# A two-layer decoder trunk in 32-bit split arithmetic: attention scores issued at another place, and the norm's row made by plain 32-bit matmuls

## The chip, the cores and the metric

The kernel runs on one NeuronCore of one Trainium2 chip. The metric is the device time of one launch in microseconds (us), as the median of several executions. All times below are in us unless they are marked ns. Engines go by the short names of the profile: PE is TensorE (matmuls), PEld its weight loads, DVE is VectorE, ACT is ScalarE, POOL is GpSimd, SP is SyncE, which issues the DMAs.

## The reference

One sequence of 256 tokens, width 2048, two layers, everything in float32:

```python
for i in range(2):
    a = rmsnorm(h, attn_norm[i])
    h = h + (sb_dilated_mixer if i == 0 else fox_mixer)(a, ...)      # 16 heads of 128
    h = h + conv_ffn(rmsnorm(h, ffn_norm[i]), ...)                   # 2048 -> 2*5632 -> 2048
    gate = sigmoid(rmsnorm(h, ple_norm[i]) @ w_ple_gate[i])
    h = h + gate * (p[i] @ w_ple[i])
return rmsnorm(h, final_norm)
```

Layer 0 has 8 stick-breaking heads (the weight of a key is a product of the "not taken" shares of the keys after it, computed with a suffix sum) and 8 dilated heads with rotary positions (softmax). Layer 1 has 16 forgetting heads (softmax with a bias from cumulated forget gates).

## The kernel before, in words

**The arithmetic.** A 32-bit weight is split in two float32r parts: ACT copies it rounded (L165), DVE subtracts that copy from the original (L166). Activations are kept in two such parts as well. A product of the two takes three float32r matmuls per 128 x 128 block (`PARTS`: high by high, high by low, low by high). Small matmuls of attention take their operands as plain float32 instead and are recorded twice in the trace for each matmul.

**The stream of weights.** All weights come through one list, cut into units of mostly 4 blocks of 128 rows by 256 columns. SP loads groups of units into the raw tile `wr` (3 buffers), ACT and DVE split a unit into `w` (4 buffers), PE uses it in 24 matmuls of 256 columns. `unit` keeps three split units ahead of PE.

**The order of the work.** `gemm_unit` and `gemm_v` call `tick()` after every unit. `defer(n, fn)` puts a small job into a list that `tick` runs n units later, so that attention stands between units of the large products. A scheduler then orders the instructions on each engine, on the whole as they were written.

**A head pair** (`head_pair`, 8 per layer) makes the queries (`psq`, 4 units, weights stationary, activations moving), the keys (`psk`, 4 units, likewise) and the values (`psv`, 4 units; `gemm_v` at L229 to L240, where the activations are stationary and the weights move). Its attention has three steps that PE takes part in: `first` makes the scores `scs` (stick-breaking: L428, L431 in `sb_first`; softmax: L472, L474, and in layer 1 also L470, in `sm_first`); `second`, 5 units later (stick-breaking, L450 to L455) or 4 units later (softmax, the transposes of L509), makes `sps`; `attend`, 2 units after that, makes `avp` (L518, L520). Between the three, DVE and ACT work on the scores: masks, exponentials, sums. In layer 1 each pair is followed by one short unit, `psp` (12 matmuls, weights stationary, `ple_up`). The first pair of layer 1 makes its values first, together with the forget gates (`gemm_vf`, L250).

In the kernel before, `first` is deferred by 2 units after the keys, or by 3 in layer 0 where rotary positions have to be applied (pairs 4 to 7). So the scores stand inside the four units of `psv`, at the half or after the third unit. In the first pair of layer 1, where no `psv` follows, they stand in the next `psq` instead.

**The norm.** `norm_sums` adds the squares over partitions by matmuls (`nps`, L291) and finds the factor per token, `rT`, by small DVE steps. `norm_rows` spreads it as a row over all partitions: the identity times `rT` (`nd`, L314) is multiplied by a matrix of ones into `rps`, and DVE copies the row to `rb` (L325). Before the change, six of the seven norms split `nd` in two float32r parts, `ndh` by ACT (L321) and `ndl` by DVE (L322), and add two float32r matmuls of 256 columns (L324). The last norm (`mixer is None`) takes two plain 32-bit matmuls of 128 columns each (L316).

Of the kernel before, what the change touches and what calls it, by code (L numbers as in the profile page):

```python
# [10 lines left out]
F32 = mybir.dt.float32  # L11
F32R = mybir.dt.float32r
# [5 lines left out]
P = 128  # L18
D = 2048
S = 256  # L20
# [36 lines left out]
def _cuts(n):  # L57
    return (4, 4, n // 2 - 4, n // 2 - 4) if n != 16 else (4, 4, 4, 4)
# [46 lines left out]
def trunk(ctx: ExitStack, tc: tile.TileContext, xT, pT, pos, gains, conv, bf, cst, wst, out):  # L105
    nc = tc.nc
# [19 lines left out]
    ones = ct[:, C_ONE:C_ONE + 128]  # L126

    def mm_tile(name):
        return psum.tile([P, 2, S], F32, name=name, tag="mm", bufs=4)

    def at_tile(name):
        return psum.tile([P, 2, 512], F32, name=name, tag="at", bufs=2)

    def t2_tile(name, shape=(P, 2, S), dt=F32):
        return work.tile(list(shape), dt, name=name, tag="t2", bufs=6)
# [46 lines left out]
    def defer(n, fn):  # L182
        later.append((at["tick"] + n, fn))
# [24 lines left out]
    def gemm(ps, act, kind, l, c0, cuts, k0=0, koff=0, part=None):  # L208
        n = len(cuts)
        for i, kc in enumerate(cuts):  # L210
            if part is None or i in part:
                gemm_unit(ps, act, kind, l, c0, k0, i == 0, i == n - 1, koff)
            k0 += kc
# [28 lines left out]
    def gemm_vf(ps, act, l):  # L242

        n = 256 + NH
        for k0, kc in VF_CUTS:
            _, w = unit("w_vf", l, k0, 2 * D)
            for t in range(2):
                for k in range(kc):
                    for i, (a, b) in enumerate(((0, 0), (0, 1), (1, 0))):
                        nc.tensor.matmul(ps[:, t, :n], lhsT=act[:, k0 + k, a, t * P:(t + 1) * P],  # L250
                                         rhs=w[:, k, b, :], start=k0 + k + i == 0,
                                         stop=k0 + k == KT - 1 and i == 2)
            tick()
# [55 lines left out]
    def norm_rows(mixer):  # L309

        dg = t2_tile("nd", (P, 2, P))
        ps = at_tile("rps")
        for t in range(2):
            nc.vector.tensor_scalar_mul(out=dg[:, t, :], in0=ident, scalar1=rT[:, t:t + 1])  # L314
            if mixer is None:
                nc.tensor.matmul(ps[:, 0, t * P:(t + 1) * P], lhsT=ones, rhs=dg[:, t, :],  # L316
                                 start=t == 0, stop=True, skip_group_check=True)
        if mixer is None:
            return ps[:, 0, :S]
        dh, dl = t2_tile("ndh", (P, 2, P), F32R), t2_tile("ndl", (P, 2, P), F32R)  # L320
        nc.scalar.copy(out=dh, in_=dg)  # L321
        nc.vector.tensor_sub(out=dl, in0=dg, in1=dh.bitcast(F32))  # L322
        for i, x in enumerate((dh, dl)):
            nc.tensor.matmul(ps[:, 0, :S], lhsT=trir[:, 0, :], rhs=x, start=i == 0, stop=i == 1)  # L324
        nc.vector.tensor_copy(out=rb, in_=ps[:, 0, :S])  # L325
        if mixer:
            nc.vector.tensor_scalar_mul(out=rq, in0=rb, scalar1=SCALE)
# [6 lines left out]
    def with_rows(fn):  # L334

        if at["rows"] > at["tick"]:
            later.append((at["rows"], fn))
        else:
            fn()
# [30 lines left out]
    trir = cpool.tile([P, 2, P], F32R, name="trir")  # L370
# [76 lines left out]
    def sb_second(z, e, eh, el):  # L447
        sp = at_tile("sps")
        for i, x in enumerate((eh, el)):
            nc.tensor.matmul(sp[:, 0, :], lhsT=trir[:, 1, :], rhs=x[:, 0:512],  # L450
                             start=i == 0, stop=False, skip_group_check=True)
            nc.tensor.matmul(sp[:, 1, 0:256], lhsT=trir[:, 1, :], rhs=x[:, 512:768],
                             start=i == 0, stop=i == 1, skip_group_check=True)
        for i, x in enumerate((eh, el)):
            nc.tensor.matmul(sp[:, 0, :].rearrange("p (j c) -> p j c", j=2)[:, :, 128:256],  # L455
                             lhsT=trir[:, 0, :], rhs=x[:, 512:768].rearrange("p (j c) -> p j c", j=2),
                             start=False, stop=i == 1, skip_group_check=True)
        nc.vector.tensor_sub(out=z, in0=z, in1=sp.rearrange("p a b -> p (a b)")[:, :768])
        nc.scalar.activation(out=e, in_=z, func=AF.Exp)
        return e  # L460
# [107 lines left out]
    def head_pair(l, hp, act, dst, st):  # L568
        q = work.tile([P, 2, S], F32, name="q", tag="qkv", bufs=2)
        k = work.tile([P, 2, S], F32, name="k", tag="qkv", bufs=2)  # L570
        v = work.tile([P, 2, S], F32, name="v", tag="v", bufs=1)
        full = _cuts(KT)
        if l % 2 == 1 and hp == 0:
            ps = at_tile("psv")
            gemm_vf(ps, act, l)
            for t in range(2):
                nc.scalar.activation(out=v[:, t, :], in_=ps[:, t, 0:S], func=AF.Copy,
                                     scale=rT[:, t:t + 1])
            st["fox"] = forget_gates(l, ps)
        ps = mm_tile("psq")  # L580
        gemm(ps, act, "w_in", l, hp * 256, full)
        with_rows(lambda ps=ps: nc.vector.tensor_mul(out=q, in0=ps, in1=rq2))
        ps = mm_tile("psk")
        gemm(ps, act, "w_in", l, D + hp * 256, full)
        nc.vector.tensor_mul(out=k, in0=ps, in1=rb2)

        def first():
            if l % 2 == 0 and hp < 4:
                a = sb_first(q, k)
                defer(5, lambda: second(lambda: sb_second(*a)))  # L590
            else:
                a = sm_first(q, k, st["fox"] + (2 * hp,) if l % 2 == 1 else None)
                defer(4, lambda: second(lambda: sm_second(*a)))

        def second(fn):
            w = fn()
            defer(2, lambda: attend(hp, w, v, dst))

        if l % 2 == 0 and hp >= 4:
            rope(q)  # L600
            rope(k)
        defer(2 + (l % 2 == 0 and hp >= 4), first)
        if l % 2 == 1 and hp == 0:
            return
        ps = mm_tile("psv")
        gemm_v(ps, act, l, 2 * D + hp * 256)
        for i in range(2):
            nc.scalar.activation(out=v[:, i, :], in_=ps[:, i, :], func=AF.Copy, scale=rT[:, i:i + 1])
# [29 lines left out]
    for l in range(DEPTH):  # L638
# [51 lines left out]
        for op in range(8):  # L690
            end = l + 1 == DEPTH and op == 7
            if end:
                ws = [unit("w_ple_gate", l, 4 * i, op * 256)[1] for i in range(4)]
                ps = [at_tile("pse")[:, j, :S] for j in range(2)]
            else:
                ps = mm_tile("psg")
# [15 lines left out]
            else:  # L712
                more = []
                for j in range(2):
                    for k in range(KT):
                        for n, (a, b) in enumerate(((0, 0), (0, 1), (1, 0))):
                            nc.tensor.matmul(ps[j],  # L717
                                             lhsT=ws[k // 4][:, k % 4, a, j * P:(j + 1) * P],
                                             rhs=X[:, k, b, :], start=k == 0 and n == 0,
                                             stop=k == KT - 1 and n == 2)  # L720
# [98 lines left out]
```

## Time and profile before

| | |
|---|---|
| median of 3 runs | 2430.46 (2429.55 to 2431.67) |
| the profiled execution's own time | 2430.3 |
| its span, first to last instruction | 2428.5 |
| PE busy | 2406.8 (99%), 20974 matmuls |
| DVE, ACT busy | 1595.8 (66%), 1228.6 (51%) |
| DMA | 458.06 MB, mean 189 GB/s |

The page's busy time of PE counts the modelled length of matmuls that overlap one another (276 ns each in the psu group), so it is not the rate at which they follow. The timeline merges the matmuls of one line into a row with the start of the first, the time to the end of the last, and their count; the difference between the starts of two rows that follow each other, divided by the count of the first, is the time that one matmul took of PE.

### The profile page before, as it was taken

The page shows a single profiled execution, that of the slowest core. Times are in us where ns is not written, and L with a number is a line of the kernel's source. Part 1 is how long each engine was busy: PE and PEld are TensorE (multiplying, and loading weights), DVE is VectorE, ACT ScalarE, POOL GpSimd, SP SyncE. Part 2 cuts the span into 40 slices and gives each one's busy share as a digit, 9 for nine tenths or more (in the row PEclk, how much of TensorE's full clock was granted, in tenths as well). Part 3 has the DMA queues.
Part 4 walks back from the last instruction along what each step waited for, and adds up shares of the span by engine and source line. Part 5 has one row for each costly group of instructions (what it writes and reads, how often), then busy time and mean ns, then how long its engine had stood idle before and what let it go on. Part 6 is the DMA issues. An engine that isn't in the chain of part 4 may idle for free.

```text
span 2428.5 us, 47969 instructions
## 1 busy us (share of the span) xinstructions
PE 2406.8 (99%) x20974; PEld 2400.7 (99%) x20974; DVE 1595.8 (66%) x2157; ACT 1228.6 (51%) x1549; POOL 2.5 (0%) x8
## 2 busy tenths in 40 slices
PE   8999999999999999999999999999999999999997
PEld 8999999999999999999999999999999999999997
DVE  7557666776567657767765555667665776667676
ACT  6554455554355445555554444555544554455553
POOL 0000000000000000000000000000000000000000
PEclk9999999999999999999999999999999999999998
DMA  7444445555555555555455445555555555555553
GB/s 269 174 174 174 170 178 191 192 195 198 197 191 191 187 200 196 197 185 204 176 184 181 170 170 167 199 191 198 193 191 192 193 198 191 201 191 187 193 196 120
DMA packets 66484, 458.06 MB, mean 189 GB/s; under 512 B 7409, under 2 KB 7425, under 8 KB 16609
## 3 DMA queue, kind: packets, MB, share of 16 engines
q1 hardware_dynamic: 66096, 454.53, 53.0%
q8 instruction: 164, 2.69, 0.4%
q0 software_dynamic: 176, 0.46, 0.1%
q14 instruction: 48, 0.39, 0.0%
HBM read 452.86 MB, written 2.10 MB: 187 GB/s over the span
## 4 chain that ended last, share of the span: by engine, by line
PE 98%; DVE 1%; DMA 1%; issue 0%; ACT 0%; SPq 0%; DVEq 0%; ACTq 0%
PE psu L203 39%; PE psd L203 20%; PE pso L203 7%; PE psk L203 7%; PE psq L203 7%; PE psv L237 7%; PE psg L203 7%; DMA wr<-in_w 1%; PE avp L518 1%; PE psp L203 0%; PE pse L717 0%; PE scs L474 0%; PE psv L250 0%; PE sps L509 0%; PE avp L520 0%
## 5 line engine op out<-in xcount | busy, mean ns | idle before, releaser
L166 DVE TENSOR_TENSOR w<-wr,w 128x1024 fp32r<-128x1024 f32 (+2 forms) x882 | 1051.9, 1193 | 694.4 <-ACT w L165 686.8
L165 ACT CAST w<-wr 128x1024 fp32r<-128x1024 f32 (+2 forms) x882 | 905.4, 1028 | 1080.4 <-PE psu L203 353.5
L203 PE MATMUL psu<-act,w 128*128 128x256 f32 x8448 | 959.3, 276 | 0.0
L203 PEld LDWEIGHTS psu<-act,w 128*128 128x128 f32 x8448 | 958.3, 188 | 0.0
L203 PE MATMUL psd<-act,w 128*128 128x256 f32 x4224 | 479.7, 276 | 0.0
L203 PEld LDWEIGHTS psd<-act,w 128*128 128x128 f32 x4224 | 479.2, 188 | 0.0
L203 PE MATMUL psq<-act,w 128*128 128x256 f32 x1536 | 185.7, 280 | 1.2 <-DVE w L166 1.2
L203 PEld LDWEIGHTS psq<-act,w 128*128 128x128 f32 x1536 | 180.3, 188 | 1.8 <-DVE w L166 1.6
L203 PE MATMUL psk<-act,w 128*128 128x256 f32 x1536 | 179.8, 277 | 0.0
L203 PEld LDWEIGHTS psk<-act,w 128*128 128x128 f32 x1536 | 176.5, 188 | 0.0
L203 PE MATMUL pso<-act,w 128*128 128x256 f32 x1536 | 175.8, 277 | 0.0
L203 PEld LDWEIGHTS pso<-act,w 128*128 128x128 f32 x1536 | 174.9, 188 | 0.0
L237 PE MATMUL psv<-w,act 128*128 128x256 f32 x1440 | 173.3, 279 | 0.0
L237 PEld LDWEIGHTS psv<-w,act 128*128 128x128 f32 x1440 | 169.0, 188 | 0.6
L203 PE MATMUL psg<-act,w 128*128 128x256 f32 x1440 | 164.4, 276 | 0.0
L203 PEld LDWEIGHTS psg<-act,w 128*128 128x128 f32 x1440 | 163.7, 188 | 0.0
L617 DVE TENSOR_TENSOR u<-psu,rb 128x512 f32<-128x512 f32 x88 | 60.9, 692 | 33.3 <-PE psu L203 33.2
L623 DVE SCALAR_TENSOR_TENSOR yv<-u,cv,yv 128x256 f32<-128x256 f32 x176 | 73.4, 480 | 0.0
L623 DVE SCALAR_TENSOR_TENSOR yg<-u,cv,yg 128x256 f32<-128x256 f32 x176 | 73.4, 480 | 0.0
L620 ACT ACTIVATE yg<-u,cv 128x256 f32<-128x256 f32 x88 | 48.1, 594 | 1.0 <-DVE u L617 1.0
L620 ACT ACTIVATE yv<-u,cv 128x256 f32<-128x256 f32 x88 | 48.1, 594 | 0.0
L261 ACT CAST act<-yg 128x512 fp32r<-128x512 f32 x44 | 27.4, 622 | 39.2 <-DVE yg L633 39.2
(172 smaller groups left out, 881.7 us busy)
## 6 DMA issues: line engine op xcount, KB each, us to landing
wr<-in_w SPq DMA_DIRECT2D x388, 1024.0 KB, 4.8
wr<-in_w SPq DMA_DIRECT2D x36, 768.0 KB, 4.3
wr<-in_w SPq DMA_DIRECT2D x8, 896.0 KB, 4.7
wr<-in_w SPq DMA_DIRECT2D x7, 512.0 KB, 6.4
h<-in_x SPq DMA_DIRECT2D x4, 512.0 KB, 6.8
out_dram<-h SPq DMA_DIRECT2D x8, 256.0 KB, 2.4
wr<-in_w SPq DMA_DIRECT2D x2, 816.0 KB, 4.4
ct<-in_c SPq DMA_DIRECT2D x1, 841.0 KB, 7.8
```

Of the source, the lines that this page charges most:

```text
L165: nc.scalar.copy(out=w[:, :, 0, :], in_=raw)
L166: nc.vector.tensor_sub(out=w[:, :, 1, :], in0=raw, in1=w[:, :, 0, :].bitcast(F32))
L203: nc.tensor.matmul(ps[:, j, :], lhsT=w[:, k, s, js], rhs=act[:, k0 - koff + k, t, :], start=first and j + k + n == 0, stop=last and k == k ...
L237: nc.tensor.matmul(ps[:, t], lhsT=act[:, 4 * i + k, a, tsl], rhs=w[:, k, b], start=i + t + k + n == 0, stop=i == 3 and k == kc - 1 and n = ...
L261: nc.scalar.copy(out=dst[:, :, 0, :], in_=src)
L518: nc.tensor.matmul(av[:, 0, j * S:(j + 1) * S], lhsT=v[:, 0, js], rhs=w[:, j * S:(j + 1) * S], start=j == 0, stop=False, skip_group_check= ...
L617: nc.vector.tensor_mul(out=u[:, :, 2:], in0=ps, in1=rb2)
L620: nc.scalar.activation(out=y[:, j, :], in_=u[:, j, 2:], func=AF.Identity, bias=cv[:, l, t, 3:4], scale=cv[:, l, t, 2:3])
L623: nc.vector.scalar_tensor_tensor(out=y[:, j, :], in0=u[:, j, tap:tap + S], scalar=cv[:, l, t, tap:tap + 1], in1=y[:, j, :], op0=ALU.mult, ...
```

## The change

Two edits. The first takes away the parts of the norm's row: all seven norms now use the two plain 32-bit matmuls of 128 columns, and ACT's copy, DVE's subtraction and the two float32r matmuls of 256 columns go. The second defers the scores by 4 units instead of 2 or 3, which puts them between the pair's last unit of `psv` and what follows (`psq` of the next pair, or `psp` in layer 1). `second` and `attend` follow at the same distances as before. The last pair of each layer and the first pair of layer 1 keep their places, so 13 of 16 pairs are moved.

```diff
         for t in range(2):
             nc.vector.tensor_scalar_mul(out=dg[:, t, :], in0=ident, scalar1=rT[:, t:t + 1])
-            if mixer is None:
-                nc.tensor.matmul(ps[:, 0, t * P:(t + 1) * P], lhsT=ones, rhs=dg[:, t, :],
-                                 start=t == 0, stop=True, skip_group_check=True)
+            nc.tensor.matmul(ps[:, 0, t * P:(t + 1) * P], lhsT=ones, rhs=dg[:, t, :],
+                             start=t == 0, stop=True, skip_group_check=True)
         if mixer is None:
             return ps[:, 0, :S]
-        dh, dl = t2_tile("ndh", (P, 2, P), F32R), t2_tile("ndl", (P, 2, P), F32R)
-        nc.scalar.copy(out=dh, in_=dg)
-        nc.vector.tensor_sub(out=dl, in0=dg, in1=dh.bitcast(F32))
-        for i, x in enumerate((dh, dl)):
-            nc.tensor.matmul(ps[:, 0, :S], lhsT=trir[:, 0, :], rhs=x, start=i == 0, stop=i == 1)
         nc.vector.tensor_copy(out=rb, in_=ps[:, 0, :S])
...
-        defer(2 + (l % 2 == 0 and hp >= 4), first)
+        defer((2 + (l % 2 == 0 and hp >= 4) if hp == 7 or (l % 2 == 1 and hp == 0) else 4), first)
```

On PE, the second head pair of layer 0 (stick-breaking) stood so before, from its values to the third step of its attention:

```order
L237 MATMUL psv<-w,act_68 128x256 x48
L428 MATMUL scs<-q,k 128x256 x2
L431 MATMUL scs<-q,k 128x128 x2
L237 MATMUL psv<-w,act_68 128x256 x48
L203 MATMUL psq<-act_68,w 128x256 x72
L450 MATMUL sps<-eh,trir 128x512
```

and stands so now:

```order
L237 MATMUL psv<-w,act_68 128x256 x96
L422 MATMUL scs<-q,k 128x256 x2
L425 MATMUL scs<-q,k 128x128 x2
L203 MATMUL psq<-act_68,w 128x256 x96
L203 MATMUL psk<-act_68,w 128x256 x24
L444 MATMUL sps<-eh,trir 128x512
```

The scores have left the 96 matmuls of `psv`, and 120 matmuls of 256 columns still stand between them and `sps`.

In layer 1 the scores move in the same way, from the half of `psv` to its end, with `psp` next behind them and 84 matmuls up to `sps` as before.

On DVE, the softmax of a middle pair of layer 1 stood so before (`s` the masked scores, `mx` the maxima, `rsm` the reciprocal sums, `pe` the shares, which the transposes `sps` take):

```order
L483 SCALAR_TENSOR_TENSOR s<-scs,cq_13741,ct 128x256
L483 SCALAR_TENSOR_TENSOR s<-scs,cq_13741,ct 128x128
L483 SCALAR_TENSOR_TENSOR s<-scs,cq_13741,ct 128x256
L490 TENSOR_REDUCE mx<-s 128x2 x2
L496 RECIPROCAL rsm<-sm 128x4
L499 TENSOR_SCALAR pe<-pe,rsm 128x128 x2
L499 TENSOR_SCALAR pe<-pe,rsm 128x256 x2
L166 TENSOR_TENSOR w<-wr,w 128x4x256 x6
```

and stands so now:

```order
L477 SCALAR_TENSOR_TENSOR s<-scs,cq_13725,ct 128x256
L477 SCALAR_TENSOR_TENSOR s<-scs,cq_13725,ct 128x128
L477 SCALAR_TENSOR_TENSOR s<-scs,cq_13725,ct 128x256
L484 TENSOR_REDUCE mx<-s 128x2 x2
L166 TENSOR_TENSOR w<-wr,w 128x4x256 x2
L490 RECIPROCAL rsm<-sm 128x4
L493 TENSOR_SCALAR pe<-pe,rsm 128x128 x2
L493 TENSOR_SCALAR pe<-pe,rsm 128x256 x2
L166 TENSOR_TENSOR w<-wr,w 128x4x256 x3
```

Two splits of weights have come between the maxima and the reciprocals, so they stand inside the chain that `sps` waits for. In the stick-breaking pairs one split more stands ahead of `el` (two in the first pair), in the dilated pairs one between the masked scores and the maxima.

On PE, in the keys of the launch's first head pair, the first norm's row stood so before (the parts 50 and 58 matmuls behind the sums of squares `nps`, and the rest of the keys behind them):

```order
L291 MATMUL nps<-ct,acc 128x2 x2
L203 MATMUL psk<-act_68,w 128x256 x50
L324 MATMUL rps<-ndh,trir 128x256
L203 MATMUL psk<-act_68,w 128x256 x8
L324 MATMUL rps<-ndl,trir 128x256
L203 MATMUL psk<-act_68,w 128x256 x26
```

and stands so now:

```order
L291 MATMUL nps<-ct,acc 128x2 x2
L203 MATMUL psk<-act_68,w 128x256 x45
L315 MATMUL rps<-nd,ct 128x128 x2
L203 MATMUL psk<-act_68,w 128x256 x39
L237 MATMUL psv<-w,act_68 128x256 x96
```

The row's matmuls come 5 matmuls earlier there and stand together. (Lines below the edits are numbered 6 lower in the changed kernel until the second edit, 5 lower behind it.)

## The prediction

> **What bounds the kernel.** I read the page first, then the chain that ended last, then PE's waits, and then the timeline of PE through one head pair of each kind.
>
> ```profile
> PE 2406.8 (99%) x20974; PEld 2400.7 (99%) x20974; DVE 1595.8 (66%) x2157; ACT 1228.6 (51%) x1549; POOL 2.5 (0%) x8
> ...
> PE 98%; DVE 1%; DMA 1%; issue 0%; ACT 0%; SPq 0%; DVEq 0%; ACTq 0%
> ```
>
> PE is busy for 99% of the span and carries 98% of the chain. DVE has a third of its time free, ACT half.
>
> ```profile
> ACT w L165 <- PE psu L203: 353.5, 266, 2.1
> ...
> PE psq L203 <- DVE w L166: 1.2, 2, 1.0
> ...
> PE rps L324 <- ACT ndh L321: 0.5, 2, 0.3
> ```
>
> The waits say the same (who waited for whom: us in total, times, longest). The splitting of weights waits for PE to free a buffer, 353.5 us behind psu alone; PE waited for a split twice in its query products, 1.2 us together. So taking work from DVE or ACT gives nothing by itself. A change gains only if PE gets fewer cycles to do, waits less for a norm's row (0.5 us in all), or takes its matmuls at a faster rate. The page can't show the last, since its busy time overlaps. The starts in the timeline of PE can. This is the first head pair:
>
> ```profile
> 46.65 5.61 PE L237 MATMUL psv<-w,act 128*128 128x256 f32 x48
> 52.10 1.02 PE L428 MATMUL scs<-q,k 128*128 128x256 f32 x4
> ...
> 53.32 5.90 PE L237 MATMUL psv<-w,act 128*128 128x256 f32 x48
> 59.06 8.64 PE L203 MATMUL psq<-act,w 128*128 128x256 f32 x72
> 67.54 0.39 PE L450 MATMUL sps<-eh,trir 128*128 128x512 f32 x1
> ...
> 74.36 0.38 PE L520 MATMUL avp<-e,v 128*128 128x128 f32 x2
> 74.58 0.60 PE L518 MATMUL avp<-e,v 128*128 128x256 f32 x2
> 75.01 0.38 PE L520 MATMUL avp<-e,v 128*128 128x128 f32 x2
> 75.15 8.44 PE L203 MATMUL psk<-act,w 128*128 128x256 f32 x72
> 83.42 0.84 PE L237 MATMUL psv<-w,act 128*128 128x256 f32 x6
> ```
>
> Ahead of the scores, 48 value matmuls take 52.10 - 46.65 = 5.45 us, 113.5 ns each. Behind them, 48 take 59.06 - 53.32 = 5.74 us, and the next 72, queries, take 67.54 - 59.06 = 8.48 us, 117.8 ns each. No row has a wait. Behind avp, which is a block of plain 32-bit matmuls too, the pace is lost for a moment only: 72 keys take 83.42 - 75.15 = 8.27 us, which is 0.10 more than 72 x 113.5 ns. So there is a fast and a slow pace, 4.3 ns apart. The value product, which holds activations and streams weights, doesn't come back to the fast one behind a block of 32-bit matmuls; the queries that follow inherit the slow one, until sps; a product that holds weights does come back.
>
> The same in the dilated pairs, where the scores stand behind the third unit of values:
>
> ```profile
> 203.03 3.17 PE L237 MATMUL psv<-w,act 128*128 128x256 f32 x24
> 206.04 8.65 PE L203 MATMUL psq<-act,w 128*128 128x256 f32 x72
> 214.53 0.82 PE L509 MATMUL sps<-ct,pe 128*128 128x128 f32 x6
> ```
>
> From the scores' end to sps, 96 matmuls take 214.53 - 203.03 = 11.50 us. The trace has one pair whose scores stand in a product that holds weights, the first of layer 1:
>
> ```profile
> 1253.67 8.54 PE L203 MATMUL psq<-act,w 128*128 128x256 f32 x72
> 1262.05 2.89 PE L203 MATMUL psk<-act,w 128*128 128x256 f32 x24
> 1264.77 0.82 PE L509 MATMUL sps<-ct,pe 128*128 128x128 f32 x6
> ```
>
> There 96 matmuls behind the same kind of block take 1264.77 - 1253.67 = 11.10 us. The other pairs of layer 1 look so:
>
> ```profile
> 1281.87 6.01 PE L237 MATMUL psv<-w,act 128*128 128x256 f32 x48
> 1287.71 1.54 PE L203 MATMUL psp<-pact,w 128*128 128x256 f32 x12
> 1289.08 2.89 PE L203 MATMUL psq<-act,w 128*128 128x256 f32 x24
> 1291.81 0.82 PE L509 MATMUL sps<-ct,pe 128*128 128x128 f32 x6
> ```
>
> The values behind the scores take 5.84 us, 0.39 over the clean 5.45; psp takes 1.37 and the queries behind it 2.73 for 24, so the pace is back. From scores to sps it is 9.94 us for 84 matmuls.
>
> **The scores' place, term by term.** Each moved pair keeps its matmuls and their number between scores and sps. What changes is which product follows the scores: psq or psp, which hold weights. I price this with the row of the kind that comes back.
>
> Stick-breaking, pairs 0 to 3: before, 120 matmuls from 53.32 to 67.54, 14.22 us. After, 72 as those behind avp (8.27, whose last matmul has 128 columns as the scores' last has) and 48 clean ones (5.45): 13.72. Gain 0.50 each, 2.0 for four.
>
> Dilated, pairs 4 to 6: 11.50 before, 11.10 as in the pair of layer 1. Gain 0.40 each, 1.2 for three.
>
> Forgetting, pairs 1 to 6 of layer 1: 9.94 before; after, the 11.10 less 12 clean matmuls (12 x 113.5 ns = 1.36), 9.74. Gain 0.20 each, 1.2 for six.
>
> Together 4.4 us. The bounds: nothing, if the pace doesn't come back, and 5.7 if even the 0.10 that is lost behind a block went in all 13 pairs (1.3 more). I take 4.4, since the scores of layer 1's first pair, which have a product that holds weights behind them, are the nearest rows.
>
> The Trainium skill speaks against this term: its page "TensorE: Matmul & The Clock Gate", under "Back-to-back issue gap", gives the isolated spacing of warm matmuls by their columns alone, N/2.4 + 2.5 ns, an estimate of 109.2 ns at 256 columns, and by it the place of the scores is worth nothing. The trace disagrees with both halves: the rows have 113.5 and 117.8 ns for the same shape.
>
> **What hides the rest of the move.** DVE and ACT keep the same work, at other places between the splits. PE would feel it if sps came too early for the chain on the scores.
>
> ```profile
> 99.99 0.95 DVE L444 TENSOR_TENSOR el<-e,eh 128x768 fp32r<-128x768 f32 x1
> ```
>
> ```profile
> 104.31 0.39 PE L450 MATMUL sps<-eh,trir 128*128 128x512 f32 x1
> ```
>
> ```profile
> 1286.67 1.01 DVE L499 TENSOR_SCALAR pe<-pe,rsm 128x128 f32<-128x128 f32 x4
> 1287.60 1.21 DVE L166 TENSOR_TENSOR w<-wr,w 128x1024 fp32r<-128x1024 f32 x1
> ```
>
> In the second pair the last step on DVE ends at 100.94, 3.37 us ahead of its sps at 104.31; in layer 1 at 1287.68, 4.13 ahead of 1291.81. In the changed order two more splits stand inside the chain of layer 1 between the maximum and the reciprocal, 1.21 us each. That leaves 4.13 - 2.42 = 1.7 us, so the cover holds and the term is nothing. In the stick-breaking pairs one split more stands ahead of el, which leaves 3.37 - 1.21 = 2.2; the first pair has two more, and what it could miss there is one split, 1.2 once, which the range has room for. SP's transfers stand in the same order as before, and PE frees the weights' buffers as before, so nothing moves there. If the cover were gone, a missed 1.21 us would cost that much per pair: the third rival.
>
> **The norm's row.** The first norm, from its sums on:
>
> ```profile
> 36.20 5.92 PE L203 MATMUL psk<-act,w 128*128 128x256 f32 x50
> 42.42 0.39 PE L324 MATMUL rps<-ndh,trir 128*128 128x256 f32 x1 [0.30 <-ACT ndh L321]
> 42.64 1.09 PE L203 MATMUL psk<-act,w 128*128 128x256 f32 x8
> 43.57 0.28 PE L324 MATMUL rps<-ndl,trir 128*128 128x256 f32 x1
> 43.69 3.13 PE L203 MATMUL psk<-act,w 128*128 128x256 f32 x26
> ```
>
> ```profile
> 41.45 0.48 DVE L314 TENSOR_SCALAR nd<-ct,rT 128x128 f32<-128x128 f32 x2
> ```
>
> 58 keys and both parts take 43.69 - 36.20 = 7.49 us, 0.91 over 58 x 113.5 ns = 6.58. Now PE comes to the row after 45 keys, at about 36.20 + 45 x 0.1135 = 41.3, and finds nd's first half ready only about 41.7 (its two halves end by 41.93): 0.4 of waiting, then two 32-bit matmuls of 128 columns. One takes 74.58 - 74.36 = 0.22 ahead of another and 75.15 - 75.01 = 0.14 ahead of a float32r one, which then pays the 0.10 of lost pace: 0.46. Together 0.86 against 0.91: no change. The norm in layer 1's first values waits for ndh likewise and gets the same value. The other four don't wait:
>
> ```profile
> 418.67 0.28 PE L324 MATMUL rps<-ndh,trir 128*128 128x256 f32 x1
> 418.85 0.39 PE L324 MATMUL rps<-ndl,trir 128*128 128x256 f32 x1
> 419.07 2.11 PE L203 MATMUL psu<-act,w 128*128 128x256 f32 x17
> ```
>
> There the two parts take 0.40 and the two 32-bit matmuls 0.46: 0.06 more each at most, 0.2 for four, of which I count 0.1 because the parts will lose some pace too. Bounds for all six: 0.3 gained (the wait of the two gone) to 0.5 lost. ACT's copy and DVE's subtraction lie beside PE's work and save nothing.
>
> **The sum.** 4.4 - 0.1 = 4.3 us less than the profiled execution's 2430.3, which is 0.16 below the median of the runs shown, 2430.46. The median should come to 2426.1 (0.18% less).
>
> **The rivals.** First: the slow pace belongs to that stretch of the program (to the values' second half and the queries) and not to the scores ahead of it. Then nothing is gained: 2430.5. For it: psq is slow without any block ahead of it but slow psv. Against it: the first half of psv is fast, and so are the queries of layer 1 behind psp. Chance 0.10. The rule of the Trainium skill above would give this time.
>
> Second: queries right behind scores stay slow until sps as they do behind slow values, while psp comes back as it does now. Then the seven pairs of layer 0 gain nothing and the six of layer 1 their 1.2: 2429.3. For it: the 72 queries at 59.06 had every chance to come back and didn't. Against it: the 72 at 1253.67. Chance 0.10.
>
> Third, on the other side: the chain on the scores comes late for sps. In the six pairs of layer 1 it now contains two splits, and each split waits in turn for PE to free a buffer, a unit apart (24 x 113.5 ns = 2.7 us). If that puts the end 1.2 us behind sps, six pairs lose 1.2 each, 7.3 together, against 4.3: 3.0 slower, 2433.5. It decides from 4.13 us of delay on; the two splits explain 2.4. Chance 0.04.
>
> **How the numbers follow.** The forecast keeps 0.76. Its own range is 2424.8 to 2427.4: down by the 1.3 of the scores' upper bound, up by the one split that the first pair could miss. The scatter of the runs, about 1 either way of the median, is of the same size. To hold 8 in 10 the range takes in the second rival as well: 2424.8 to 2429.3; the first and the third, 0.14, stay out. A measurement of this kernel can tell about 0.2% from no change, 4.9 us, so the border of faster is 2425.6. It lies inside the forecast's own range, and a third of the 0.76 falls below it: 0.25. The rest of it and the first two rivals are within 0.2%: 0.71. Slower is the third rival: 0.04.
>
> **What would show it.** In the changed kernel's timeline 96 values should take about 10.9 us without a break, and from the scores to sps the 120 matmuls of pairs 0 to 3 about 13.7, the 96 of pairs 4 to 6 about 11.1, the 84 of layer 1 about 9.7. The last pair of each layer keeps its slow stretch. The row's matmuls should show a wait for nd of about 0.4 in the first norm. I am wrong if the queries behind the scores run at 117.8 ns, or if PE's waits name el or pe ahead of sps.

## The result, and the profile after

| | before | after |
|---|---|---|
| median (lowest to highest of 4 runs each) | 2430.11 (2429.55 to 2431.67) | 2490.18 (2490.04 to 2490.76) |
| the profiled execution's own time | 2430.3 | 2490.76 |
| its span | 2428.5 | 2489.0 |

After over before is 1.0247, with a 95% interval of 1.0234 to 1.026: the change makes the kernel 60 us slower. The forecast was 2426.1, in a range of 2424.8 to 2429.3. It was wrong.

The page of the changed kernel reads much as before, PE at 99%:

```profile
PE 2468.5 (99%) x20986; PEld 2462.3 (99%) x20986; DVE 1593.4 (64%) x2151; ACT 1225.2 (49%) x1543; POOL 2.5 (0%) x8
...
L203 PE MATMUL psu<-act,w 128*128 128x256 f32 x8448 | 995.9, 281 | 0.0
```

The group of the MLP's first product stood so in the page of before:

```profile
L203 PE MATMUL psu<-act,w 128*128 128x256 f32 x8448 | 959.3, 276 | 0.0
```

As many matmuls, no idle time, but 5 ns more for each, by the page's modelled ends. A change in so small a mean, over a product that no edit touches, is the trail. The waits of the changed kernel name no engine that PE has begun to wait for in the MLPs: the splits wait longer for PE (392.8 us behind psu, 353.5 before), and PE's longest wait is for the first split at the launch, 5.4 (5.9 before).

```profile
ACT w L165 <- PE psu L203: 392.8, 267, 2.1
```

Next comes a window well inside layer 0's MLP, where nothing but psu and psd runs. The columns are the stretch and its length, busy time and count of PE, PEld, DVE, ACT and POOL, the granted clock, the DMA share and GB/s. Before:

```profile
420.00:770.00 350.00, 350.00 (x3091) 350.00 (x3090) 235.29 (x311) 176.64 (x204) 0.00 (x0) 1.00 0.55 194
```

After:

```profile
420.00:770.00 350.00, 350.00 (x2974) 350.00 (x2973) 224.73 (x296) 169.14 (x196) 0.00 (x0) 1.00 0.52 187
```

PE is busy for the whole of both, at a granted clock of 1.00 in both. But 350 us hold 3091 matmuls before and 2974 after: 113.23 and 117.69 ns each, 4.46 apart. These are the two paces that the prediction found among the head pairs. After the change the MLP runs at the slow one. The Trainium skill's page "TensorE: Matmul & The Clock Gate", under "Back-to-back issue gap", gives the spacing of an isolated matmul by its columns alone (an estimate of 109.2 ns at 256, worked out from its formula). The same product of 256 columns at the same clock has two spacings here, and the measurement decides.

Where the slow pace starts and ends is read from the starts of the norm's blocks in PE's timeline, the row `rps` and the next norm's sums `nps`. Before (the first row, at 418.67, stands in the prediction):

```profile
1131.73 0.50 PE L291 MATMUL nps<-ct,acc 128*128 128x2 f32 x4
1137.63 0.28 PE L324 MATMUL rps<-ndh,trir 128*128 128x256 f32 x1
...
1218.22 0.59 PE L291 MATMUL nps<-ct,acc 128*128 128x2 f32 x4
...
1619.69 0.28 PE L324 MATMUL rps<-ndh,trir 128*128 128x256 f32 x1
...
2332.76 0.50 PE L291 MATMUL nps<-ct,acc 128*128 128x2 f32 x4
2338.66 0.28 PE L324 MATMUL rps<-ndh,trir 128*128 128x256 f32 x1
...
2412.53 0.50 PE L291 MATMUL nps<-ct,acc 128*128 128x2 f32 x4
```

After:

```profile
412.84 5.70 PE L203 MATMUL psu<-act,w 128*128 128x256 f32 x48
418.38 0.60 PE L315 MATMUL rps<-nd,ct 128*128 128x128 f32 x4
...
1159.41 0.50 PE L291 MATMUL nps<-ct,acc 128*128 128x2 f32 x4
...
1165.32 0.60 PE L315 MATMUL rps<-nd,ct 128*128 128x128 f32 x4
...
1248.82 0.59 PE L291 MATMUL nps<-ct,acc 128*128 128x2 f32 x4
...
1649.01 0.60 PE L315 MATMUL rps<-nd,ct 128*128 128x128 f32 x4
...
2390.04 0.50 PE L291 MATMUL nps<-ct,acc 128*128 128x2 f32 x4
2395.95 0.60 PE L315 MATMUL rps<-nd,ct 128*128 128x128 f32 x4
...
2472.71 0.50 PE L291 MATMUL nps<-ct,acc 128*128 128x2 f32 x4
```

From the row to the next sums:

| stretch | before | after | more |
|---|---|---|---|
| MLP, layer 0 | 713.06 | 741.03 | 27.97 |
| gates, layer 0 | 80.59 | 83.50 | 2.91 |
| MLP, layer 1 | 713.07 | 741.03 | 27.96 |
| gates, layer 1 | 73.87 | 76.76 | 2.89 |

Together 61.7. Each MLP has 6336 matmuls (8448 of psu and 4224 of psd over two layers), 48 of them ahead of the row; the other 6288 times 4.46 ns make 28.0. So every matmul from the row on is slow, until the sums of the next norm. Ahead of the row the 48 are fast (418.38 - 412.84 = 5.54, some 0.1 of it behind the sums). The spans differ by 60.5, so elsewhere 1.2 is gained.

That is in layer 1: from the sums at 1218.22 to the row at 1619.69 it was 401.47 before, and from 1248.82 to 1649.01 it is 400.19. The second pair and the first dilated pair of layer 0, and a pair of layer 1, in the changed kernel's timeline:

```profile
83.14 11.05 PE L237 MATMUL psv<-w,act 128*128 128x256 f32 x96
94.02 1.02 PE L422 MATMUL scs<-q,k 128*128 128x256 f32 x4
...
95.25 11.55 PE L203 MATMUL psq<-act,w 128*128 128x256 f32 x96
...
109.47 0.39 PE L444 MATMUL sps<-eh,trir 128*128 128x512 f32 x1
...
205.46 11.66 PE L203 MATMUL psq<-act,w 128*128 128x256 f32 x96
216.96 0.82 PE L503 MATMUL sps<-ct,pe 128*128 128x128 f32 x6
...
1317.90 1.73 PE L203 MATMUL psp<-pact,w 128*128 128x256 f32 x12
1319.47 8.33 PE L203 MATMUL psq<-act,w 128*128 128x256 f32 x72
1327.63 0.82 PE L503 MATMUL sps<-ct,pe 128*128 128x128 f32 x6
```

The values are whole and fast (94.02 - 83.14 = 10.88 for 96). From the scores' end to sps it is 14.22 in the stick-breaking pair and 11.50 in the dilated one, the same as before to the hundredth: the queries, which hold weights, stay slow. In layer 1, where psp follows, it is 9.73 against 9.94.

### The profile page after: what moved, and what is told of

Read it like the earlier page. It is cut to its first block, busy times and chain, and to the rows that moved or that the text cites. A ratio compares the mean times of both kernels' runs of the same rounds, so it can differ in the third digit from the quotient of the medians.

```text
span 2489.0 us, 47978 instructions
## 1 busy us (share of the span) xinstructions
PE 2468.5 (99%) x20986; PEld 2462.3 (99%) x20986; DVE 1593.4 (64%) x2151; ACT 1225.2 (49%) x1543; POOL 2.5 (0%) x8
## 4 chain that ended last, share of the span: by engine, by line
PE 98%; DVE 1%; ACT 0%; issue 0%; DMA 0%; SPq 0%; DVEq 0%
PE psu L203 40%; PE psd L203 20%; PE pso L203 7%; PE psk L203 7%; PE psg L203 7%; PE psq L203 7%; PE psv L237 7%; PE avp L512 1%; PE psp L203 1%; PE psv L250 0%; PE pse L712 0%; PE scs L468 0%; PE sps L503 0%; DMA wr<-in_w 0%; PE avp L514 0%
## 5 line engine op out<-in xcount | busy, mean ns | idle before, releaser
L165 ACT CAST w<-wr 128x1024 fp32r<-128x1024 f32 (+2 forms) x882 | 903.8, 1025 | 1145.3 <-PE psu L203 392.8
L203 PE MATMUL psu<-act,w 128*128 128x256 f32 x8448 | 995.9, 281 | 0.0
L203 PEld LDWEIGHTS psu<-act,w 128*128 128x128 f32 x8448 | 994.7, 189 | 0.0
L203 PE MATMUL psd<-act,w 128*128 128x256 f32 x4224 | 498.5, 281 | 0.0
L203 PEld LDWEIGHTS psd<-act,w 128*128 128x128 f32 x4224 | 497.9, 189 | 0.0
L203 PE MATMUL psg<-act,w 128*128 128x256 f32 x1440 | 170.5, 281 | 0.0
L203 PEld LDWEIGHTS psg<-act,w 128*128 128x128 f32 x1440 | 169.6, 189 | 0.0
L237 PE MATMUL psv<-w,act 128*128 128x256 f32 x1440 | 166.7, 276 | 0.0
L269 ACT ACTIVATE act<-h,gn 128x256 fp32r<-128x256 f32 x96 | 43.5, 503 | 2.3 <-DMA h<-in_x 1.4
```

The costliest lines, as they stand in the source:

```text
L165: nc.scalar.copy(out=w[:, :, 0, :], in_=raw)
L203: nc.tensor.matmul(ps[:, j, :], lhsT=w[:, k, s, js], rhs=act[:, k0 - koff + k, t, :], start=first and j + k + n == 0, stop=last and k == k ...
L237: nc.tensor.matmul(ps[:, t], lhsT=act[:, 4 * i + k, a, tsl], rhs=w[:, k, b], start=i + t + k + n == 0, stop=i == 3 and k == kc - 1 and n = ...
L269: nc.scalar.activation(out=dst[:, k, 0, :], in_=h[:, k, :], func=AF.Copy, scale=gn[:, g, k:k + 1])
```

## The experiments

The theory after the result (A): two plain 32-bit matmuls of 128 columns, back to back, switch PE to the slow pace, also in a product that holds weights, and nothing brings it back until another small block comes. Its rivals: the tiles and work that went with the parts, or their buffers, make the difference (B); the scores at their new place do (C). Where a kernel keeps "the row by parts", it has the lines that the first edit took away.

**Each edit alone.** One kernel has only the scores moved (`e1`: the kernel before with the second edit), one only the row changed (`e2`). `e2` against the changed kernel:

```diff
-        defer((2 + (l % 2 == 0 and hp >= 4) if hp == 7 or (l % 2 == 1 and hp == 0) else 4), first)
+        defer(2 + (l % 2 == 0 and hp >= 4), first)
```

> Only the scores are moved; the norm's row is made by float32r parts as before the change. Theory A (pace): the 60 us come from the norm's row alone, because two plain 32-bit matmuls of 128 columns leave PE at 117.8 ns per matmul and nothing ends that for a whole MLP. Then this kernel is near the one before: the queries behind the scores in layer 0 stay slow (no gain), layer 1 gains 0.2 us in each of six pairs, so about 2429 us. Theory B (buffers): the row's two tiles that went shift the rotation of the small work tiles; they are back here, so also about 2429. Theory C (scores): the moved scores cost the 60 us: about 2490.

Measured: 2428.99 against 2429.99 for the kernel before, ratio 0.9996 (0.9987 to 1.0004).

> Only the norm's row is changed; the scores stand where they stood before. Theory A (pace): about 2491 us, with 113.3 ns per MLP matmul ahead of each row and 117.8 behind it until the next block of small matmuls. Theory B (buffers): about 2491 as well. Theory C (scores): about 2430.

Measured: 2491.85 against 2429.99, ratio 1.0254 (1.0239 to 1.027). The row makes all of the loss, and C falls.

**Two float32r matmuls behind the row.** `e2`, and behind the row what looks like the old pair:

```diff
+        for i in range(2):
+            nc.tensor.matmul(ps[:, 1, :S], lhsT=trir[:, 0, :], rhs=trir.rearrange("p a b -> p (a b)"),
+                             start=i == 0, stop=i == 1, skip_group_check=True)
```

> As the kernel with only the norm's row changed, and behind the row's two 32-bit matmuls stand two float32r matmuls of 256 columns into a PSUM bank that nobody reads. Theory A (pace): the last block decides, and float32r matmuls of 256 columns are what stood there before, so the MLP runs at 113.3 ns again and the time is about 2431 us (some 0.25 us more work in each of six norms). Theory B (buffers): the work tiles lie as in the changed kernel, so about 2491 us and 117.8 ns in the MLP.

Measured: 2493.53 against 2429.99, ratio 1.0261 (1.0247 to 1.0275). Not what A expected with its addition that such a pair brings the fast pace: the MLP stays slow. The next run says why.

**A probe.** Between all units of the MLPs of the kernel before (in layer 1 in the middle of units too) stands one of 13 small blocks (one of them empty), drawn at random; their results are not read.

> The kernel before, with small blocks of matmuls on constants put into both MLPs, results unread: in layer 0 at the end of every unit, in layer 1 in the middle of every unit (between the two halves of the output), drawn at random from 13 kinds: two or one float32r matmuls of 256 columns; one float32r of 128; two or one plain 32-bit of 128; one of 256; four of 256, 128, 256, 128; four of 128, 256, 128, 256; four of 256, 256, 128, 128; six transposes; two of 2 columns; two times float32r 256, 32-bit 128, 32-bit 256; none. The time says nothing, the pace of the matmuls behind each block does. Theory A (pace): behind two plain matmuls of 128 columns 117.8 ns, behind two float32r of 256 columns 113.3 ns, and with none the pace of before goes on, whichever it was; a kind's answer is the same at nearly all of its places. Theory B (buffers): the pace does not follow the blocks.

Its whole time, 2814.14, says nothing. From the trace I counted the pace behind each block by the starts of the matmuls up to the next block (slow: over 115.5 ns apart). `f` is a plain 32-bit matmul, `r` a float32r one, 1 and 2 stand for 128 and 256 columns:

```
block               from the fast pace    from the slow pace
none                stays fast            stays slow
f1                  fast 41 of 41 (from either)
f1 f1               slow 35 of 35         fast 15 of 17
f2                  slow 27 of 27         fast  2 of 15
r1                  fast 38 of 38 (from either)
r2                  slow 28 of 28         fast  8 of 12
r2 r2               slow 19 of 19         slow 13 of 13
f2 f1 f2 f1         fast 46 of 46 (from either)
f1 f2 f1 f2         fast 51 of 51 (from either)
f2 f2 f1 f1         fast 40 of 40 (from either)
r2 f1 f2 r2 f1 f2   fast 25 of 25         fast 14 of 17
six transposes      slow 16 of 27         fast 13 of 14
two of 2 columns    slow 26 of 26         fast  9 of 13
```

So the two matmuls of the new row, `f1 f1`, turn the fast pace into the slow one 35 times in 35, in a product that holds weights. Two back-to-back float32r matmuls of 256 columns with the same weights do so too; that is what `e3` added, and it goes against A's addition. A single `f1` or `r1` always left the fast pace here. The blocks `f1 f2 f1 f2` and `f2 f2 f1 f1` have the columns of the dilated and of the stick-breaking scores, and leave the fast pace too, although the scores themselves were followed by slow queries. This gave the next four runs.

**A block that resets, behind the row.** `e2`, with one `r1` of unread result one unit later:

```diff
+    def pace_block():
+        t = at_tile("pl")
+        nc.tensor.matmul(t[:, 0, 0:P], lhsT=trir[:, 0, :], rhs=trir[:, 0, :],
+                         start=True, stop=True, skip_group_check=True)
...
+        defer(6, pace_block)
```

> Only the norm's row is changed (scores where they stood), and one unit behind each row stands one float32r matmul of 128 columns, its result unread; in the probe all 38 blocks of this kind were followed by 113.3 ns, whatever pace was ahead. Theory A (pace, set by the last block): 24 slow matmuls per row instead of some 3100, so about 2431 us (2430.0 + 6 x 0.2). Theory B (buffers of the work tiles shifted by the two tiles that went): 117.8 ns in the MLP as before it, about 2492 us.

Measured: 2432.01 against 2430.33, ratio 1.0007 (0.9998 to 1.0016). Its timeline at the first MLP:

```profile
420.09 3.08 PE L203 MATMUL psu<-act,w 128*128 128x256 f32 x24
423.00 0.22 PE L325 MATMUL pl<-trir 128*128 128x128 f32 x1
```

and the window behind it:

```profile
780.00:1120.00 340.00, 340.00 (x3002) 340.00 (x3001) 226.70 (x296) 172.08 (x209) 0.00 (x0) 1.00 0.55 194
```

24 matmuls take 2.91 behind the row, 121 ns each; behind the one small matmul the MLP runs at 340/3002 = 113.3 ns. It has the new row, without parts and their tiles, and one matmul more at each row, and of the 61.9 us only 1.7 are left. B falls.

**The same two matmuls, one unit apart.** The row's halves are made by two jobs, at 5 and 6 units (the two functions are left out here):

```diff
...
-        defer(5, lambda: norm_rows(mixer))
+        defer(5, one)
+        defer(6, two)
```

> The norm's row by the same two plain 32-bit matmuls of 128 columns, but one unit (24 matmuls) apart, and what waits for the row waits one unit longer; scores where they stood. In the probe one such matmul alone was followed by 113.3 ns at all 41 places, two together by 117.8 at all 35 places that were fast ahead. Theory A (pace): 2430 us, give or take 1. Theory B (buffers): about 2492, since the work tiles are allocated as in the kernel with only the row changed. Theory D (plain 32-bit matmuls of constants with these weights are slow for what follows, whatever their number): about 2492.

Measured: 2430.49 against 2430.33, ratio 1.0001 (0.9992 to 1.0011). The arithmetic of the changed kernel's row, to the matmul, at the time of the kernel before:

```profile
419.19 0.38 PE L319 MATMUL rps<-nd,ct 128*128 128x128 f32 x2
419.32 2.98 PE L203 MATMUL psu<-act,w 128*128 128x256 f32 x24
422.15 0.38 PE L319 MATMUL rps<-nd,ct 128*128 128x128 f32 x2
```

The 24 between take 2.83. What costs 60 us is that the two stand together.

**The block in the kernel before.** The other direction: before, with one `f1 f1` of unread result in the middle of layer 0's MLP.

```diff
+        if l == 0:
+            defer(136, pace_block)
```

> The kernel before with one block more: two plain 32-bit matmuls of 128 columns on constants, results unread, once, at the middle of the MLP of layer 0. Nothing else is changed, no tile of the work pool either. Theory A (pace): the 3144 matmuls up to the next block (the sums of squares of the next norm) take 4.45 ns more each, 14.0 us, so 2430.0 + 0.4 + 14.0 = 2444.4 us. Theory B (buffers): 2430.4.

Measured: 2444.68 against 2430.33, ratio 1.0059 (1.0045 to 1.0073), 14.35 us for a block that takes PE 0.36 in the timeline:

```profile
776.09 0.60 PE L332 MATMUL pc<-ct 128*128 128x128 f32 x4
776.45 8.73 PE L203 MATMUL psu<-act,w 128*128 128x256 f32 x72
```

The window behind it:

```profile
780.00:1120.00 340.00, 340.00 (x2890) 340.00 (x2889) 217.40 (x282) 164.50 (x200) 0.00 (x0) 1.00 0.53 185
```

It holds 2890 matmuls, 340/2890 = 117.6 ns each, where the same window of `e6` holds 3002. Ahead of the block, 420 to 770 holds 3091 as in the kernel before, 113.2 ns each. DVE, ACT and DMA do less behind it than in `e6`'s window (217.40 against 226.70, 164.50 against 172.08, 185 GB/s against 194), as PE takes fewer weights in the same time.

**The scores with a reset.** `e1`, with the `r1` of above one unit behind the scores in layer 0 (the same `pace_block`, deferred by 1 from the scores).

> Scores moved, norm's row by float32r parts as before the change (this alone gave 2429.0), and in layer 0 one float32r matmul of 128 columns, its result unread, one unit behind the scores of each pair. Theory A (pace): the queries behind it run at 113.3 ns; 96 of 120 matmuls of pairs 0 to 3 and 72 of 96 of pairs 4 to 6 and of the last pair are won at 4.45 ns each, less 0.13 for the block: 4 x 0.30 + 4 x 0.19 = 2.0, so 2427.0 us. Rival: the queries of layer 0 are slow for another reason than the scores ahead of them (their place in the program), then 2430 us (eight blocks more).

Measured: 2427.33 against 2430.33, ratio 0.9987 (0.9979 to 0.9996). In the second pair:

```profile
95.51 3.08 PE L203 MATMUL psq<-act,w 128*128 128x256 f32 x24
98.42 0.22 PE L331 MATMUL pl<-trir 128*128 128x128 f32 x1
98.48 8.39 PE L203 MATMUL psq<-act,w 128*128 128x256 f32 x72
106.71 1.52 PE L203 MATMUL psk<-act,w 128*128 128x256 f32 x12
```

The 24 behind the scores take 2.91, the 72 behind the small matmul 8.23, 114.3 each. From the scores to sps it is 13.93 against 14.22, and in the dilated pairs 11.31 against 11.50: some 1.7 of the 3.2 that were forecast for layer 0, which the scores' place alone doesn't give. In the last pair of layer 0, where the block stands between the values and `pso`, it did not bring the fast pace back: the 72 matmuls behind it take 8.54.

**Which part of a block decides.** A second probe, with 14 blocks, between "the whole block decides" (N) and "its last matmul decides" (L).

> The probe again with other blocks (results unread; the time says nothing): one, two, three and four plain 32-bit matmuls of 128 columns; two, three and four of 256; two and three float32r of 128; two of 128 with two different weights; 128 then 256 and 256 then 128; two of 128 and then a float32r of 128; two float32r of 256 and then one of 128. Known from the first probe: one of 128 is followed by the fast pace always, two by the slow one where it was fast ahead, one of 256 by the slow one mostly, four of mixed widths by the fast one. Theory N (the block as a whole shifts PE's two queues against each other): the answer changes with the number, three or four of one form answer otherwise than two, and two with different weights may differ from two with the same. Theory L (the last matmul decides): three and four of 128 answer as two, and what ends with one float32r matmul of 128 is followed by 113.3 ns always, as that block alone was (38 of 38).

```
block               from the fast pace    from the slow pace
f1                  fast 22 of 22         fast 18 of 18
f1 f1               slow 21 of 21         fast 11 of 13
f1 f1 f1            fast 18 of 18         fast 17 of 17
f1 f1 f1 f1         slow 21 of 21         fast 13 of 15
f2 f2               fast 20 of 20         fast 18 of 18
f2 f2 f2            slow 28 of 28         fast 16 of 17
f2 f2 f2 f2         slow 27 of 27         slow 18 of 18
r1 r1               fast 20 of 20         fast 17 of 17
r1 r1 r1            fast 22 of 22         slow 15 of 17
f1 f1, two weights  slow 30 of 30         fast 12 of 12
f1 f2               slow 33 of 33         fast 16 of 17
f2 f1               fast 27 of 27         fast 12 of 12
f1 f1 r1            slow 18 of 18         fast 15 of 16
r2 r2 r1            fast 19 of 19         fast  9 of 9
```

L falls: one, two, three and four of the same matmul differ, and `f1 f1 r1` ends as `r1` does, which always gave the fast pace alone. N stands in that the whole block decides; several blocks turn the pace over, whichever it was, and `f1 f2` and `f2 f1` show that the order counts. That PE's two queues are shifted against each other is N's picture of the cause; no run shows it.

**Both edits, kept fast.** The scores moved with `e9`'s block in pairs 0 to 6 of layer 0, the row's halves apart as in `e8`.

> Both edits of the change in a form that keeps the pace: scores moved, one unread float32r matmul of 128 columns one unit behind the scores of pairs 0 to 6 of layer 0 (with the row in parts, and one block more, this gave 2427.33), and the norm's row by two plain 32-bit matmuls one unit apart (alone 2430.49, against 2430.33 before). Theory A (pace): the two effects add, 2427.3 + 0.2 - 0.1 = 2427.4 us. Rival: the pace depends on the whole program's alignment and the two don't add, then anything from 2427 to 2490, with slow stretches in the MLP.

Measured: 2427.64 against 2430.12, ratio 0.999 (0.9981 to 0.9999). The two effects add.

**The scores in another order.** `e1`, with the score matmuls of layer 0 ordered 256, 128, 256, 128 columns, a series that the probe found fast 46 times in 46 (as it did the orders that the scores have without this edit, 40 in 40 and 51 in 51, so a block's columns were already known not to decide alone). In the dilated pairs:

```diff
...
+            for t in ((1, 0) if fox is None else (0, 1)):
+                nc.tensor.matmul(sc[:, j, 128 * t:128 + 256 * t], lhsT=q[:, j, t * P:(t + 1) * P],
...
```

> Scores moved, norm's row by float32r parts (2429.0 so far), no block added; only the order of the four score matmuls of layer 0 is changed to 256, 128, 256, 128 columns in all its pairs (before: 256, 256, 128, 128 in the stick-breaking ones and 128, 256, 128, 256 in the dilated ones). The value product avp has that order and the keys behind it were fast in all 16 pairs of the kernel before. Theory N (a block's form decides the pace behind it): the queries of layer 0 come back to 113.3 ns, a gain of 2.0 in the stick-breaking pairs and 1.2 to 1.6 in the dilated ones, so about 2425.6 us. Rival (the first product behind a block decides: a new group of queries, which starts a PSUM tile, doesn't come back, keys in the middle of their group do): 2429.0 us, queries at 117.8 ns.

Measured: 2428.93 against 2430.69, ratio 0.9994 (0.9985 to 1.0003): the time of `e1`, a miss for N. (Behind `avp` the kernel before has keys in 8 of its 16 pairs, queries in 6 and `pso` in 2; all run fast.) The queries behind the scores stayed slow:

```profile
95.90 11.55 PE L203 MATMUL psq<-act,w 128*128 128x256 f32 x96
...
110.12 0.39 PE L449 MATMUL sps<-eh,trir 128*128 128x512 f32 x1
```

110.12 - 95.90 = 14.22 again. So the order of the columns does not decide alone. Whether the place does is asked next.

**The scores inside the queries.** `e1`, with the scores of layer 0 one unit later still, so that they stand behind the first unit of the next queries:

```diff
-        defer((2 + (l % 2 == 0 and hp >= 4) if hp == 7 or (l % 2 == 1 and hp == 0) else 4), first)
+        defer((2 + (l % 2 == 0 and hp >= 4) if hp == 7 or (l % 2 == 1 and hp == 0) else 4 + (l == 0)), first)
```

> Scores moved one unit further in layer 0 (pairs 0 to 6): behind the first unit of the next pair's queries, with the rest of the steps at their distances; layer 1 as moved, norm's row by float32r parts, no block added. Rival of the last run (the first product behind a block decides): in the middle of a group of queries the pace comes back, as behind the scores of layer 1's first pair and behind avp in the keys, so all of psv and psq but some 5 matmuls run at 113.3 ns: 2429.0 less 2.0 and 1.2, about 2425.8 us. Theory N (a block's form decides, and these scores are a slow form wherever they stand): 120 and 96 matmuls stay slow, 2429.0 us.

Measured: 2427.82 against 2430.41, ratio 0.9989 (0.998 to 0.9998), 2.0 above the rival's time. The first pair's queries and scores, then the second pair:

```profile
57.89 2.99 PE L203 MATMUL psq<-act,w 128*128 128x256 f32 x24
60.72 1.02 PE L428 MATMUL scs<-q,k 128*128 128x256 f32 x4
...
83.26 11.56 PE L237 MATMUL psv<-w,act 128*128 128x256 f32 x96
94.66 2.90 PE L203 MATMUL psq<-act,w 128*128 128x256 f32 x24
97.39 1.02 PE L428 MATMUL scs<-q,k 128*128 128x256 f32 x4
...
98.62 8.42 PE L203 MATMUL psq<-act,w 128*128 128x256 f32 x72
...
112.32 0.39 PE L450 MATMUL sps<-eh,trir 128*128 128x512 f32 x1
```

The same scores, unchanged, are now followed by fast queries: 120 in 112.32 - 98.62 = 13.70, the very 13.7 of the prediction. But the later steps move along, avp now stands ahead of the values, and these run slow behind it (94.66 - 83.26 = 11.40 against 10.88 for 96). That takes back most of it in the four stick-breaking pairs.

The rows show one thing more: the pace can turn where one product follows another, with no block between. In the first pair the 24 queries ahead of the scores are slow (60.72 - 57.89 = 2.83, 117.9 ns each) right behind values that run at the fast pace (96 from 47.00 to 57.89, 10.89). In the second they are fast (97.39 - 94.66 = 2.73) right behind slow values. So it is in this run at all three places of the first kind and all four of the second; in the kernel before, slow values are followed by slow queries, so it is no rule either. So A's "nothing brings it back until another small block comes" holds inside the MLPs, but not everywhere. And the slow queries of `e1` may come from the start of the queries rather than from the scores; no run separates the two.

## Why the prediction was wrong, point by point

**The step that failed** is the norm's row, "+0.1", bounded by 0.3 gained and 0.5 lost. It measured 61.7 in four stretches (61.9 in `e2`). Its price for the block itself was near: the same two matmuls take PE 0.36 in `e10` (776.45 - 776.09), as 0.22 and 0.14 had it. What it counted as "the 0.10 of lost pace" behind the block was a lasting loss of 4.46 ns on each of 6288 matmuls in each MLP and 648 in each of the gates.

**The premise under it** was that "a product that holds weights does come back". It was a rule made from three places where one did, avp ahead of keys, the scores of layer 1's first pair and psp. The first probe set 35 blocks of the row's form into products that hold weights and ran fast, and behind not one of them did they come back. The prediction even had the counterexample in a row, the 72 queries at 59.06, and read it as inherited from the values; nothing in the rows that it shows tells values and queries apart in this. The bound should have been taken from that row: if the pace can last over 120 matmuls without a way back, it could last over 6288, and 6288 x 4.3 ns is 27 us. The norm's row stands ahead of the longest unbroken stretches in the program, where the same uncertainty of 4 ns weighs most; I gave it the smallest term.

**The scores' place.** The second rival was right: queries right behind scores stay slow (14.22 and 11.50 as before), psp comes back. Layer 1 gave 0.21 in the pair shown, 0.20 forecast; layer 0 gave nothing of its 3.2. `e1`'s ratio cannot tell 1 us from none, the trace can. The rival's time, 2429.3, lies 0.3 above what `e1` measured (2428.99, 1.0 below the kernel before where the rival has 1.2).

**The cover on DVE** held, with more room than forecast. In a pair of layer 1 the two splits stand inside the chain and it still ends at 1324.22, 3.4 ahead of sps at 1327.63 (1.7 forecast):

```profile
1320.52 2.36 DVE L166 TENSOR_TENSOR w<-wr,w 128x1024 fp32r<-128x1024 f32 x2
...
1323.21 1.01 DVE L493 TENSOR_SCALAR pe<-pe,rsm 128x128 f32<-128x128 f32 x4
```

No wait of PE names pe or el. The third rival, the only one on the slow side, had a mechanism that didn't occur.

**The first norm** was forecast at 0.86 over the clean pace, with a wait of 0.4 for nd:

```profile
35.75 5.54 PE L203 MATMUL psk<-act,w 128*128 128x256 f32 x45
41.38 0.52 PEld L315 LDWEIGHTS rps<-nd,ct 128*128 128x128 f32 x4 [0.29 <-DVE nd L314]
41.38 0.71 PE L315 MATMUL rps<-nd,ct 128*128 128x128 f32 x4
41.84 4.68 PE L203 MATMUL psk<-act,w 128*128 128x256 f32 x39
46.36 0.84 PE L237 MATMUL psv<-w,act 128*128 128x256 f32 x6
```

45 keys and the row take 6.09, 0.98 over 45 x 113.5 ns. The forecast's wait is there: the weight load of the row waits 0.29 for nd, and the row takes 0.46 (41.84 - 41.38). The rest is the pace. The last five keys ahead of the row start at 40.54, so the first 40 take 4.79, 119.8 ns each; the 39 behind the row take 4.52, 115.9 ns each. Both begin with a matmul of some 0.2 behind a block. So the keys run slow ahead of the row and fast behind it. That is not against the probe, in which `f1 f1` turned the slow pace into the fast one 15 times in 17. But it is no rule either: in `e2` the same row at the same place, behind slow keys as well, is followed by slow keys (39 in 4.68).

**What stays open** is the law. The pace ahead, the block's make and its place all count. The scores are followed by slow queries at the start of a group and by fast queries inside it, avp by fast keys and, in `e14`, by slow values, and the pace turns between values and queries without any block. Why the old pair of float32r matmuls kept the MLP fast is open as well. Their starts were 0.18 apart (418.67 and 418.85), against 0.11 to 0.12 in the probe's `r2 r2`; but in `e3`, behind `f1 f1`, such a pair started 0.20 apart and the MLP stayed slow. Whether the gap made the difference wasn't tried. It is not the clock (1.00 in both), not a wait of PE, not DMA, DVE or ACT, which all did less in the slow stretches.

## What to carry to other kernels

On a kernel that PE bounds, as this one, read the pace of its long products as matmuls per window (or start to start) in every stretch, not its busy share, and do so again after any edit that changes a small block between them. Where one pace is seen to last behind some block, price it over the whole stretch to the next block, and put the widest bound on the block that stands ahead of the longest stretch. If a stretch turns out slow, split the block by one unit or put one small matmul behind it: here that gave back 60 us (`e8`, `e6`), and with the scores it gave 2427.33 and 2427.64, both below the kernel before (2430.33 and 2430.12). Then read the pace again: between two products the same small matmul did nothing (`e9`, last pair of layer 0).

## What the runs showed of the hardware that was not expected

- The same stream of float32r matmuls of 256 columns runs at 113.2 or at 117.7 ns each at a granted clock of 1.00, and keeps its pace for thousands of matmuls (6288 in a row in the changed kernel) until a small block stands in it. Between values and queries it turned with no block, both ways (`e14`: 24 queries in 2.83 behind fast values, in 2.73 behind slow values).
- A block of 0.36 us turned the rest of a product slow and cost 14.35 us (`e10`); behind one float32r matmul of 128 columns it was fast 38 times in 38 in the first probe, 20 of them from slow.
- The number in a block matters in no monotonous way: one plain 32-bit matmul of 128 columns leaves the fast pace (22 of 22 from fast), two the slow one (21 of 21), three the fast one (18 of 18), four the slow one (21 of 21).
